# Feed-forward: 42 gate and up tile pairs by a seven-product scheme, two of four weight sums by adding DMAs

## The chip, the cores and the metric

The kernel runs on one core of a Trainium2 chip. The metric is the device time of one execution in microseconds. TensorE does the matmuls, ScalarE (ACT) and VectorE (DVE) the elementwise work from SBUF and PSUM, GpSimd (POOL) elementwise work from SBUF, and SyncE (SP) issues nearly all DMAs.

## What is computed

A network on 512 tokens of width 1024, three layers in a row (a gated delta rule layer, a latent attention layer, and a second block with retention and windowed attention). Each ends in a feed-forward part with 2816 hidden columns, and the change lies in these three parts alone:

```python
def swiglu(h, w_gate, w_up, w_down):
    return (jax.nn.silu(h @ w_gate) * (h @ w_up)) @ w_down
# layers 0 and 1
h = rmsnorm(x, norm_ffn_g[layer]) * (1.0 + scale_f) + shift_f
x = x + gate_f * swiglu(h, ffn_w_gate[layer], ffn_w_up[layer], ffn_w_down[layer])
# second block (layer 2 here)
h2 = rms_norm(x, ln2_g[l])
x = x + (jax.nn.silu(h2 @ w_ffn_gate[l]) * (h2 @ w_ffn_up[l])) @ w_ffn_down[l]
```

All is float32. The kernel gets its accuracy from products of split numbers: every operand is a high half (`whi`, `hhi`) and the rest (`wlo`, `hlo`), and `mm3` (L140) makes one product of three matmuls: high by high, high by low, low by high.

## The kernel before

Activations stand transposed: eight tiles `h[k]` of 128 features by 512 tokens, each as a high and a low tile. A weight panel of 1024 by 128 columns is loaded by one DMA that SP issues (`panel`, L563) into a raw buffer `wraw` (pool `wr`, 2 buffers, L344), then split in two halves of 512: ScalarE casts to `whi` (L560), VectorE subtracts to `wlo` (L561). `whi` and `wlo` have four buffers each (pool `wp`).

`ffn` (L1170) makes a list of tiles. For each of the 22 hidden tiles c there is one of gate and one of up, each 8 k-tiles by 3 matmuls of 512 columns into one PSUM bank. `gate_done` (L1177) applies silu on ScalarE; in layer 2, where the norm is applied late (`before.late`), VectorE first scales by the norm's row and GpSimd scales again after silu (L1181 to L1183). `up_done` (L1188) multiplies on VectorE (L1191) and splits the product into `ah` and `al`. Hidden tiles come in three groups of 8, 7 and 7 (FGROUPS). After each of the first two groups stand eight tiles of the down projection over that group, added to the residual `xT` on VectorE (L637, L639). The third group's down projection is `residual` (L641), whose last four tiles and the following layer's first four run in halves of 256 tokens. The first two hidden tiles of each part are made by the stage before.

`stream` (L603) runs the list: the weights of tile i+1 are asked for inside tile i. TensorE's order is the order of the program. The orders of VectorE, ScalarE, GpSimd and SP are laid out by the framework's scheduler from a plan; each engine then works through its own order and waits where its next instruction isn't ready. In the trace the weight splits run some tiles ahead, as far as the buffers reach.

In layer 0 a side job goes along: `ada` (L542) loads 56 tiles of 512 KB into two buffers `adaw` by SP (L551) and reduces each on VectorE (L554), one step every five steps of the stream (1.6 per tile). Its sums are needed by the end of layer 0's feed-forward part and later.

## Time and profile before

| | us |
|---|---|
| median of three runs (lowest, highest) | 2250.38 (2249.84, 2254.87) |
| the profiled execution, whole | 2252.93 |
| its span, first to last instruction | 2251.1 |
| TensorE busy in the span | 2164.3 |
| VectorE, ScalarE, GpSimd busy | 1281.0, 856.2, 288.9 |

The sum of a prediction is made against the profiled execution, 2252.93 us, which is 2.55 above the median. TensorE's shown durations overlap, since matmuls are pipelined: the price of one is the distance between two starts. Durations on VectorE and ScalarE overlap a little too where instructions stand back to back.

### The profile page before, as it was taken

The numbers are of one execution on the slowest core, as the hardware profiler recorded it, in microseconds if no ns is written. First come the engines' busy times: TensorE is split into PE (matmuls) and PEld (weight loads), VectorE is DVE, ScalarE is ACT, GpSimd is POOL, SyncE is SP. The second block draws the span as 40 slices with busy tenths as digits, with TensorE's granted clock in tenths as the row PEclk, the third lists the DMA queues.
The fourth block names the chain that finished last, engine by engine and source line by source line (L and its number), as shares of the span: only waits on it lengthen the run. The fifth ranks groups of instructions, "written<-read, shape, count | busy, mean of one in ns | idle before, by whom it ended". The sixth has DMA issues, their size and how long they took to land.

```text
span 2251.1 us, 30612 instructions
## 1 busy us (share of the span) xinstructions
PE 2164.3 (96%) x11532; PEld 1830.0 (81%) x11532; DVE 1281.0 (57%) x2850; ACT 856.2 (38%) x1926; POOL 288.9 (13%) x257
## 2 busy tenths in 40 slices
PE   6997989999999999999999999999999999999998
PEld 4786777888888887688888889888778889888888
DVE  7888786577653355645333337655656654434333
ACT  4663444342222244435222234333544533323223
POOL 5331000300000031012000003212111002101012
PEclk8999999899999999999999999999999999999999
DMA  7234462267763322213332333433323242332332
GB/s 278 65 105 133 129 208 87 89 205 260 244 194 97 94 62 80 66 39 106 97 101 87 106 90 92 143 97 100 93 80 103 71 129 71 115 103 89 99 98 70
DMA packets 103235, 257.56 MB, mean 114 GB/s; under 512 B 26288, under 2 KB 36016, under 8 KB 103088
## 3 DMA queue, kind: packets, MB, share of 16 engines
q1 hardware_dynamic: 100496, 252.52, 35.9%
q10 hardware_dynamic: 2592, 3.10, 0.5%
q8 instruction: 90, 1.47, 0.3%
q14 instruction: 57, 0.47, 0.1%
HBM read 240.37 MB, written 8.91 MB: 111 GB/s over the span
## 4 chain that ended last, share of the span: by engine, by line
PE 84%; DVE 8%; DMA 3%; ACT 2%; POOL 1%; issue 1%; SPq 1%; DVEq 0%; ACTq 0%; POOLq 0%
PE ps L141 20%; PE ps L143 20%; PE ps L142 20%; PE ops L141 3%; PE ops L143 3%; PE ops L142 3%; PE first L142 1%; PE first L141 1%; PE first L143 1%; DVE wlo L561 1%; DMA adaw<-in_ada_w_dram 1%; PE mo_ps L1431 1%; PE msc L1404 1%; PE so L1564 1%; PE ssc L1525 1%
## 5 line engine op out<-in xcount | busy, mean ns | idle before, releaser
L560 ACT CAST whi<-wraw 128x512 fp32r<-128x512 f32 (+3 forms) x686 | 390.2, 605 | 926.7 <-PE ps L142 421.3
L141 PE MATMUL ps<-hhi,whi 128*128 128x512 f32 x1548 | 617.0, 399 | 17.6 <-ACT graw L1008 11.4
L143 PE MATMUL ps<-hhi,wlo 128*128 128x512 f32 x1548 | 606.7, 392 | 0.2
L142 PE MATMUL ps<-hlo,whi 128*128 128x512 f32 x1548 | 605.8, 391 | 0.8 <-DVE hlo L561 0.8
L561 DVE TENSOR_TENSOR wlo<-wraw,whi 128x512 fp32r<-128x512 f32 (+3 forms) x642 | 427.3, 694 | 173.0 <-ACT whi L560 172.1
L141 PEld LDWEIGHTS ps<-hhi,whi 128*128 128x128 f32 x1548 | 292.9, 189 | 82.5 <-ACT graw L1008 11.9
L143 PEld LDWEIGHTS ps<-hhi,wlo 128*128 128x128 f32 x1548 | 292.2, 189 | 64.8 <-DVE wlo L561 3.2
L142 PEld LDWEIGHTS ps<-hlo,whi 128*128 128x128 f32 x1548 | 292.9, 189 | 59.2 <-DVE hlo L561 1.1
L223 POOL TENSOR_TENSOR acc<-acc,sq 128x512 f32<-128x512 f32 x21 | 29.8, 1426 | 909.1 <-issue 633.9
L1191 DVE TENSOR_TENSOR far<-ps,fsg 128x512 f32<-128x512 f32 x60 | 41.5, 691 | 173.9 <-PE ps L143 172.7
L141 PE MATMUL ps<-ah,whi 128*128 128x512 f32 x360 | 140.0, 389 | 0.0
L142 PE MATMUL ps<-al,whi 128*128 128x512 f32 x360 | 140.0, 389 | 0.0
L143 PE MATMUL ps<-ah,wlo 128*128 128x512 f32 x360 | 140.0, 389 | 0.0
L554 DVE CUSTOM_DVE_ANT_0 adaw<-adaw,crow 128x1024 f32<-128x1024 f32 x80 | 97.6, 1222 | 26.1 <-DMA adaw<-in_ada_w_dram 25.9
L141 PE MATMUL first<-hhi,whi 128*128 128x256 f32 (+1 forms) x336 | 102.2, 304 | 1.3 <-ACT whi L560 1.3
L142 PE MATMUL first<-hlo,whi 128*128 128x256 f32 (+1 forms) x336 | 101.0, 301 | 1.1 <-DVE hlo L260 0.7
L143 PE MATMUL first<-hhi,wlo 128*128 128x256 f32 (+1 forms) x336 | 100.0, 298 | 1.5 <-POOL wlo L561 1.5
L141 PE MATMUL ops<-ah,whi 128*128 128x256 f32 (+1 forms) x252 | 80.4, 319 | 0.0
L142 PE MATMUL ops<-al,whi 128*128 128x256 f32 (+1 forms) x252 | 79.8, 317 | 0.0
L143 PE MATMUL ops<-ah,wlo 128*128 128x256 f32 (+1 forms) x252 | 79.8, 317 | 0.0
L141 PEld LDWEIGHTS ps<-ah,whi 128*128 128x128 f32 x360 | 67.6, 188 | 14.1
L142 PEld LDWEIGHTS ps<-al,whi 128*128 128x128 f32 x360 | 67.6, 188 | 14.0
(589 smaller groups left out, 3623.6 us busy)
## 6 DMA issues: line engine op xcount, KB each, us to landing
adaw<-in_ada_w_dram SPq DMA_DIRECT2D x96, 512.0 KB, 4.5
wraw<-in_ffn_w_gate_dram SPq DMA_DIRECT2D x44, 512.0 KB, 3.5
wraw<-in_ffn_w_up_dram SPq DMA_DIRECT2D x44, 512.0 KB, 3.5
wraw<-in_w_in_dram SPq DMA_DIRECT2D x42, 512.0 KB, 3.6
wraw<-in_gdn_w_in_dram SPq DMA_DIRECT2D x32, 512.0 KB, 3.6
wraw<-in_ffn_w_down_dram SPq DMA_DIRECT2D x32, 448.0 KB, 3.3
wraw<-in_w_ffn_gate_dram SPq DMA_DIRECT2D x22, 512.0 KB, 3.5
wraw<-in_w_ffn_up_dram SPq DMA_DIRECT2D x22, 512.0 KB, 3.5
```

The lines of the kernel that those rows point to most:

```text
L141: nc.tensor.matmul(ps, whi, hhi, start=first, stop=False)
L142: nc.tensor.matmul(ps, whi, hlo, start=False, stop=False)
L143: nc.tensor.matmul(ps, wlo, hhi, start=False, stop=last)
L223: (nc.gpsimd if half is None else nc.vector).tensor_tensor(self.acc[i][:, cols], self.acc[i][:, cols], sq, op=ALU.add)
L554: nc.vector.tensor_tensor_reduce(wt, wt, self.crow, 1.0, 0.0, ALU.mult, ALU.add, raw[:, k:k + 1])
L560: self.nc.scalar.copy(dst_hi, raw)
L561: (self.nc.gpsimd if pool else self.nc.vector).tensor_tensor(dst_lo, raw, dst_hi.bitcast(F32), op=ALU.subtract)
L1191: self.behind = nc.vector.tensor_tensor(ar, ps, sg.pop(c), op=ALU.mult).ins
L1404: nc.tensor.matmul(pss[j][:, 0:nk], qn[2 * p + j][:, qs], kn[2 * p + j][:, 0:nk], start=True, stop=False)
L1431: nc.tensor.matmul(opsum[hh][:, qs], vt, pts[j][:, CS[kj]], start=kj == 0, stop=kj == qi)
L1525: nc.tensor.matmul(sc[e][:, a:z], q[rows[e], CS[b]], c.kdup[g][rows[e], (b + 1) * P - (z - a):(b + 1) * P], start=True, stop=True)
L1564: nc.tensor.matmul(o[rows[e], CS[b]], c.vt[:, kc * P + 64 * g:kc * P + 64 * g + 64], pt[e][:, y:y + P], start=y == a, stop=y + P == z)
```

## The change

42 of the 66 gate and up pairs (12, 17 and 13 of layers 0, 1 and 2, `paired`) are no longer made as two tiles of 48 matmuls of 512 columns. They are one product of 2 x 2 blocks: the blocks are gate and up in one direction, the two halves of the 1024 features in the second, the two halves of the 512 tokens in the third. Seven products of half the features and half the tokens take the place of eight, by Winograd's form of Strassen's scheme. The sums of tokens (`token_sums`) are made once per layer, in four steps, one after each of the first separate tiles. The sums of weights (`pair_weights`) are made per pair: of the four, two by DMAs that GpSimd issues and that add what they load to `u`, two by VectorE. Then g before its sums, g after, and u after are split whole (`unit`, 1024 wide), and u's second half before its sums into buffers of its own (`ffu`, two). `two` runs the seven products and combines them from PSUM. `one` runs a tile of the old kind; side steps of `ada` are taken only in these, three per tile. The raw weight buffers become four outside the first stage, the parts for tokens and outputs get pools of their own, PSUM banks are taken from the pools of three and five apart (`self.wide = False`), and the scratch for DMA descriptors that software writes is made 2048.

```diff
@@ -341,7 +341,7 @@
     def weights(self, es, n, **k):
-        self.wr, self.wp = self.pool("wr", 2, es, **k), self.pool("wp", n, es, **k)
+        self.wr, self.wp = self.pool("wr", 2 if k else 4, es, **k), self.pool("wp", n, es, **k)
...
@@ -1167,51 +1167,198 @@
+    def pair_weights(self, w1, w2, c, pool, out):
+        nc = self.nc
+        g, u = (self.wr.tile([P, KD, P], F32, name="wraw", tag="wraw") for _ in range(2))
+        for raw, w in ((g, w1), (u, w2)):
+            nc.sync.dma_start(raw, w.tiles(0, KD, c, P)[0])
+        a, b = slice(0, KD // 2), slice(KD // 2, KD)
+        def unit(raw):
+            hl = [self.wp.tile([P, 1088], F32R, name=x, tag=x)[:, 16:1040].rearrange("p (k n) -> p k n", k=KD) for x in ("whi", "wlo")]
+            self.split(*hl, raw)
+            out.append(hl)
+        unit(g)
+        hl = [pool.tile([P, 544], F32R, name=x, tag=x)[:, 16:528].rearrange("p (k n) -> p k n", k=4) for x in ("uhi", "ulo")]
+        self.split(*hl, u[:, b])
+        out.append(hl)
+        add = lambda o, x, y: nc.vector.tensor_tensor(o, x, y, op=ALU.add)
+        for o, w in ((b, w2), (a, w1)):
+            nc.gpsimd.dma_start(u[:, o], w.tiles(0, KD // 2, c, P)[0], accum_op=ALU.add)
+        add(g[:, a], u[:, b], g[:, a])
+        add(g[:, b], g[:, a], g[:, b])
+        yield
+        unit(g)
+        yield
+        unit(u)
+        yield
+    def token_sums(self, before, pool, out):
+        nc = self.nc
+        lo, hi = HALF
+        for j in range(KD // 2):
+            x = []
+            for k in (j, j + KD // 2):
+                x.append(self.nm.tile([P, T], F32, name="sq", bufs=3))
+                if before.late:
+                    nc.scalar.activation(x[-1], self.xT[k], AF.Copy, scale=before.gain[:, k:k + 1])
+                else:
+                    nc.vector.tensor_tensor(x[-1], before.h[0][k].bitcast(F32), before.h[1][k].bitcast(F32), op=ALU.add)
+            o, e = x
+            nc.vector.tensor_tensor(o[:, lo], o[:, lo], o[:, hi], op=ALU.subtract)
+            nc.vector.tensor_tensor(o[:, hi], e[:, hi], o[:, hi], op=ALU.subtract)
+            nc.vector.scalar_tensor_tensor(e[:, hi], o[:, lo], -1.0, e[:, hi], op0=ALU.mult, op1=ALU.subtract)
+            nc.vector.scalar_tensor_tensor(e[:, lo], e[:, hi], -1.0, e[:, lo], op0=ALU.mult, op1=ALU.subtract)
+            th, tl = (pool.tile([P, 4, T // 2], F32R, name=x, tag=x) for x in ("th", "tl"))
+            for i, y in enumerate(x):
+                self.split(*(a.rearrange("p i t -> p (i t)")[:, T * i:T * (i + 1)] for a in (th, tl)), y)
+            out.append((th, tl))
+            yield
     def ffn(self, l, before, first, gate, norm, firsts, side=None):
         nc, h = self.nc, before.h
         wg, wu, wd = self.ffn_weights(l)
         with ExitStack() as es:
-            fa, fs = self.pool("ffa", 8, es), self.pool("ffs", 2, es)
-            sg, a = {}, None
+            fa, ft, fs, fu = self.pool("ffa", 8, es), self.pool("fft", 4, es), self.pool("ffs", 2, es), self.pool("ffu", 2, es)
+            sg, fo, sums = {}, {}, []
+            maker = self.token_sums(before, ft, sums)
+            def gated(x):
+                if before.late:
+                    nc.scalar.activation(x, x, AF.Silu)
+                    nc.gpsimd.tensor_tensor(x, x, before.row, op=ALU.mult)
+                else:
+                    nc.scalar.activation(x, x, AF.Silu)
+            def upper(ar, a):
+                ah, al = fa.tile([P, T], F32R, name="ah"), fa.tile([P, T], F32R, name="al")
+                self.split(ah, al, ar)
+                a[0].append(ah)
+                a[1].append(al)
             def gate_done(c):
                 def done(ps):
...
-                    sg[c] = fs.tile([P, T], F32, name="fsg")
+                    fo[c] = fs.tile([P, 2, T], F32, name="fo")
+                    sg[c] = fo[c][:, 0, :]
...
-                        nc.scalar.activation(sg[c], sg[c], AF.Silu)
-                        nc.gpsimd.tensor_tensor(sg[c], sg[c], before.row, op=ALU.mult)
+                        gated(sg[c])
...
-                    ar = fs.tile([P, T], F32, name="far")
+                    ar = fo.pop(c)[:, 1, :]
-                    ah, al = fa.tile([P, T], F32R, name="ah"), fa.tile([P, T], F32R, name="al")
...
+                    upper(ar, a)
...
-            specs = []
+            def one(w, c, x, done):
+                wt = []
+                def weights():
+                    wt.append(self.cols(w, c * P))
+                    yield
+                def run():
+                    ps, n = self.ps(), w.kn
+                    for k, _ in enumerate(self.proj(ps, wt[0], x)):
+                        if side is not None and k % 3 == 1:
+                            next(side, None)
+                        if k == n // 2 - 1:
+                            yield
+                    done(ps)
+                    if x is h:
+                        next(maker, None)
+                    yield
+                return weights, run
+            def two(c, a):
+                u = []
+                lo, hi = HALF
+                def products(ps, cols, wt, at, b):
+                    for j in range(KD // 2):
+                        mm3(nc, ps[:, cols], wt[0][:, at + j, :], wt[1][:, at + j, :], *b(j), j == 0, j == KD // 2 - 1)
+                def run():
+                    B = lambda k, cols: lambda j: [x[k + j][:, cols] for x in h]
+                    S = lambda i: lambda j: [x[:, i, :] for x in sums[j]]
+                    tt = lambda o, x, y: nc.vector.tensor_tensor(o, x, y, op=ALU.add)
+                    both = lambda x: x.rearrange("p (c t) -> p c t", c=2)
+                    twice = lambda x: x.rearrange("p (c t) -> p c t", c=1).broadcast_to([P, 2, T // 2])
+                    a_, b_ = 0, KD // 2
+                    fo = fs.tile([P, 2, T], F32, name="fo")
+                    sg, ar = fo[:, 0, :], fo[:, 1, :]
+                    p15, p26, p37, p4 = self.s("p15"), self.s("p26"), self.s("p37"), self.bank("p4")
+                    products(p15, lo, u[0], a_, B(a_, lo))
+                    products(p26, lo, u[0], b_, B(b_, lo))
+                    p1 = self.nm.tile([P, T // 2], F32, name="nt", bufs=4)
+                    nc.scalar.copy(p1, p15[:, lo])
+                    yield
+                    products(p26, hi, u[2], a_, S(3))
+                    tt(fo[:, :, lo], both(p26), twice(p1))
+                    products(p37, hi, u[3], a_, S(1))
+                    products(p37, lo, u[2], b_, B(b_, hi))
+                    yield
+                    products(p15, hi, u[3], b_, S(0))
+                    x = self.nm.tile([P, T // 2], F32, name="nt", bufs=4)
+                    tt(x, p15[:, hi], ar[:, lo])
+                    tt(fo[:, :, hi], both(p37), twice(x))
+                    tt(ar[:, lo], p37[:, hi], ar[:, lo])
+                    if before.late:
+                        nc.vector.tensor_tensor(sg, sg, before.row, op=ALU.mult)
+                    gated(sg)
+                    products(p4, lo, u[1], 0, S(2))
+                    tt(ar[:, lo], p4[:, lo], ar[:, lo])
+                    self.behind = nc.vector.scalar_tensor_tensor(ar, ar, -1.0, sg, op0=ALU.mult, op1=ALU.mult).ins
+                    upper(ar, a)
+                    yield
+                return lambda: self.pair_weights(wg, wu, c * P, fu, u), run
+            todo, paired = [], self.paired(l)
             for g, (lo, hi) in enumerate(FGROUPS):
                 a = ([], [])
                 for c in range(lo, hi):
-                    specs += [(self.w(wg, c * P), h, gate_done(c)), (self.w(wu, c * P), h, up_done(c, a))]
+                    if c < len(first) // 2:
+                        gate_done(c)(first[2 * c])
+                        up_done(c, a)(first[2 * c + 1])
+                    elif c in paired:
+                        todo.append(two(c, a))
+                    else:
+                        todo += [one(wg, c, h, gate_done(c)), one(wu, c, h, up_done(c, a))]
                 if g < len(FGROUPS) - 1:
                     for n in range(KD):
-                        specs.append((self.w(wd.rows(lo, hi), n * P), a, lambda ps, n=n: self.add_to_x(n, ps, gate)))
-            for (_, _, done), ps in zip(specs, first):
-                done(ps)
-            for n, _ in enumerate(self.stream(specs[len(first):])):
-                if side is not None and n % 5 == 0:
-                    next(side, None)
+                        todo.append(one(wd.rows(lo, hi), n, a, lambda ps, n=n: self.add_to_x(n, ps, gate)))
+            self.wide = False
+            drain(todo[0][0]())
+            for i, (_, run) in enumerate(todo):
+                more = todo[i + 1][0]() if i + 1 < len(todo) else iter(())
+                next(more, None)
+                for _ in run():
+                    next(more, None)
+                drain(more)
+            self.wide = True
             if side is not None:
                 drain(side)
                 self.rope_tables(lambda name: self.nm.tile([P, T], F32, name=name, tag="sq", bufs=3))
             norm = norm()
             return norm, self.residual(wd.rows(lo, hi), a, gate, norm, firsts)
+    def paired(self, l):
+        return {c for c in range(5, 22) if l == 1 or c % (3, 0, 5)[l] != 1}
...
@@ -1851,7 +1998,7 @@
 def kernel(**inputs):
-    nc = bacc.Bacc("TRN2", target_bir_lowering=False, num_devices=1)
+    nc = bacc.Bacc("TRN2", target_bir_lowering=False, num_devices=1, dynamic_dma_scratch_size=2048)
```

## Rows read from the trace of the kernel before

**Rows 1.** The page: busy time by engine, and the chain that ended last by engine.
```profile
PE 2164.3 (96%) x11532; PEld 1830.0 (81%) x11532; DVE 1281.0 (57%) x2850; ACT 856.2 (38%) x1926; POOL 288.9 (13%) x257
...
PE 84%; DVE 8%; DMA 3%; ACT 2%; POOL 1%; issue 1%; SPq 1%; DVEq 0%; ACTq 0%; POOLq 0%
```
**Rows 2.** Windows: stretch, its length, busy us (instructions) of each engine, clock, DMA share, GB/s.
```profile
core 0: us, PE busy (x) PEld busy (x) DVE busy (x) ACT busy (x) POOL busy (x), PEclk, DMA share, GB/s
461.00:494.00 33.00, 32.91 (x147) 26.81 (x147) 26.68 (x45) 15.85 (x28) 0.00 (x0) 1.00 0.75 249
...
461.00:761.00 300.00, 299.91 (x1325) 247.90 (x1325) 177.93 (x298) 89.48 (x163) 0.00 (x0) 1.00 0.61 197
1045.00:1344.00 299.00, 298.91 (x1318) 247.03 (x1317) 111.79 (x176) 88.12 (x161) 0.00 (x0) 1.00 0.34 101
1901.00:2200.00 299.00, 299.00 (x1318) 247.05 (x1318) 122.02 (x197) 89.52 (x161) 31.82 (x22) 1.00 0.33 101
```
**Rows 3.** Timeline, TensorE: start us, duration us. First matmuls of two tiles, 24 starts apart.
```profile
1961.10 0.39 PE L141 MATMUL ps<-hhi,whi 128*128 128x512 f32 x1
...
1966.54 0.39 PE L141 MATMUL ps<-ah,whi 128*128 128x512 f32 x1
```
**Rows 4.** Timeline, TensorE, last residual: matmuls of 256 columns, 84 starts apart.
```profile
2219.50 0.28 PE L141 MATMUL ops<-ah,whi 128*128 128x256 f32 x1
...
2229.40 0.28 PE L141 MATMUL ops<-ah,whi 128*128 128x256 f32 x1
```
**Rows 5.** Timeline, TensorE, a little later: 24 starts apart.
```profile
2237.06 0.28 PE L141 MATMUL ops<-ah,whi 128*128 128x256 f32 x1
...
2239.78 0.28 PE L141 MATMUL ops<-ah,whi 128*128 128x256 f32 x1
```
**Rows 6.** Timeline, VectorE, layer 2: start us, duration us, operations back to back.
```profile
1966.81 0.69 DVE L1191 TENSOR_TENSOR far<-ps,fsg 128x512 f32<-128x512 f32 x1 [3.62 <-PE ps L143]
1967.42 1.28 DVE L561 TENSOR_TENSOR wlo<-wraw,whi 128x512 fp32r<-128x512 f32 x2
1968.62 0.69 DVE L561 TENSOR_TENSOR al<-far,ah 128x512 fp32r<-128x512 f32 x1
```
**Rows 7.** Timeline, VectorE, layer 0: a 1024-wide operation and what follows it.
```profile
468.64 1.22 DVE L554 CUSTOM_DVE_ANT_0 adaw<-adaw,crow 128x1024 f32<-128x1024 f32 x1
...
469.79 0.69 DVE L561 TENSOR_TENSOR wlo<-wraw,whi 128x512 fp32r<-128x512 f32 x1
```
**Rows 8.** Timeline, VectorE, last residual: a 256-wide operation from PSUM and what follows.
```profile
2233.06 0.42 DVE L637 TENSOR_TENSOR xT<-ops,xT 128x256 f32<-128x256 f32 x1
2233.39 0.15 DVE L538 SCALAR_TENSOR_TENSOR rstdy<-rstdt,rstdy 128x2 f32<-128x2 f32 x1
```
**Rows 9.** Groups by line, shapes apart, VectorE: count, busy us, mean ns, idle before.
```profile
L639 DVE SCALAR_TENSOR_TENSOR xT<-ps,mod,xT 128x512 f32<-128x512 f32 x32 | 24.0, 750 | 68.4 <-PE ps L143 68.4
```
**Rows 10.** Waits of VectorE, 461 to 761 us: us in total, times, longest.
```profile
DVE adaw L554 <- DMA adaw<-in_ada_w_dram: 21.9, 29, 1.5
```
**Rows 11.** Groups by line, shapes apart, VectorE, 461 to 494 us: ada reductions.
```profile
L554 DVE CUSTOM_DVE_ANT_0 adaw<-adaw,crow 128x1024 f32<-128x1024 f32 x9 | 10.9, 1222 | 1.8 <-DMA adaw<-in_ada_w_dram 1.8
```
**Rows 12.** Waits of SP's queue, 461 to 761 us.
```profile
SPq L551 <- DVE adaraw L554: 104.6, 53, 4.7
```
**Rows 13.** Timeline, SP: start us, duration us of one DMA issue.
```profile
1984.99 0.33 SPq L571 DMA_DIRECT2D wraw<-in_w_ffn_gate_dram  x1
```
**Rows 14.** Groups by line, shapes apart, GpSimd: layer 2's scaling after silu.
```profile
L1183 POOL TENSOR_TENSOR fsg<-fsg,nrow 128x512 f32<-128x512 f32 x22 | 31.8, 1448 | 284.3 <-ACT fsg L1182 284.3
```
**Rows 15.** DMA issues: count, KB each, median us from issue to landing.
```profile
adaw<-in_ada_w_dram SPq DMA_DIRECT2D x96, 512.0 KB, 4.5
...
xT<-in_xT_dram SPq DMA_DIRECT2D x8, 256.0 KB, 2.9
...
crow<-in_c_dram SPq DMA_DIRECT2D x1, 512.0 KB, 7.4
```
**Rows 16.** Timeline, ScalarE, layer 2: casts back to back.
```profile
1966.56 1.14 ACT L560 CAST whi<-wraw 128x512 fp32r<-128x512 f32 x2 [3.77 <-issue]
1967.61 0.61 ACT L560 CAST ah<-far 128x512 fp32r<-128x512 f32 x1
```

More of the change, by code (lines that the diff above doesn't have):

```diff
@@ L1189, in done @@
                 def done(ps):
-                    ar = fs.tile([P, T], F32, name="far")
+                    ar = fo.pop(c)[:, 1, :]
                     self.behind = nc.vector.tensor_tensor(ar, ps, sg.pop(c), op=ALU.mult).ins
-                    ah, al = fa.tile([P, T], F32R, name="ah"), fa.tile([P, T], F32R, name="al")
-                    self.split(ah, al, ar)
-                    a[0].append(ah)
-                    a[1].append(al)
-                return done
-            specs = []
+                    upper(ar, a)
```

## The prediction

> **What bounds the kernel now.** I read the page first, then the windows of the three feed-forward stretches, then the TensorE timeline inside them. On the page TensorE is busy 96% of the span and carries 84% of the chain that ended last [rows 1]. A share over the whole span does not say what a change in one stage is worth, so the windows come next: in each of the three gate, up and down stretches (layer 0 from 461 to 761 us, layer 1 from 1045 to 1344, layer 2 from 1901 to 2200) TensorE is busy for all but 0.1 us of 299 to 300, at clock 1.00, which is the 2.4 GHz level [rows 2]. There, and only there, the change works, and there nothing but the number and the length of the matmuls sets the time. VectorE is the next engine: 178, 112 and 122 us busy in the same windows [rows 2].
>
> The price of a matmul is the distance between starts, not its shown duration. With 512 columns, 24 starts take 1966.54 - 1961.10 = 5.44 us, 0.2267 each [rows 3]. With 256 columns, the last part of the kernel has a stretch of 84 in a row, by chance the number that a new pair has: 2229.40 - 2219.50 = 9.90 us, 0.1179 each, a little more than half of 0.2267 [rows 4]. Another stretch of the same shape, after a short break, runs at half exactly: 2239.78 - 2237.06 = 2.72 us for 24, 0.1133 each [rows 5]. What decides between the two does not show. The slow one is what followed directly on 512-column matmuls, as in the new code, so I take it.
>
> **The change on TensorE.** A gate and up pair has 2 x 8 x 3 = 48 matmuls of 512 columns: 48 x 0.2267 = 10.88 us. The new pair has 7 products of 4 k-tiles with 3 matmuls of 256 columns each, 84: 9.90 us. Saved per pair 0.98 us, for 12 + 17 + 13 = 42 pairs 41.2 us. At the quick cadence a pair takes 9.52, and 42 x 1.36 = 57.1 us are saved. Nothing covers TensorE now, so all of it is off the path, unless something else is late. The rest of the working is about that.
>
> **The change on VectorE.** Queued back to back, a 512-column tensor operation costs 0.60 us (two from 1967.42 to 1968.62), not its 0.69 [rows 6]; a 1024-column one 1.15 [rows 7]; a 256-column one that reads PSUM 0.33 [rows 8]; a scalar_tensor_tensor of 512 lasts 0.75 against 0.69, so 0.66 [rows 6, 9]. Before, a pair has four subtractions for the low halves of weights, the product of gate and up and one subtraction for its low half: 6 x 0.60 = 3.6 us, with layer 2's row scaling 4.2. After: three 1024-wide subtractions 3.45, the one for u's second half 0.60, two additions of weights 1.20; then two 512-wide and three 256-wide combinations from PSUM 1.20 + 1.00, the final product 0.66, its low half 0.60. Together 8.7 us, in layer 2 9.3. Where an operation needs the one just before it the overlap of 0.09 is lost; some four of these give 9.1 and 9.7. The pair lasts 9.9 on TensorE. So VectorE goes from 33% to over 90% of a pair: it still hides, with 0.8 us to spare in layers 0 and 1 and 0.2 in layer 2. Over a whole stretch it is well clear, since the other tiles leave it idle: 112 + 17 x 5.5 = 206 us of 282 in layer 1. In runs of pairs a wait on VectorE can therefore show. The row nearest to such a wait is that of the ada reductions, which also stand in VectorE's order for a DMA: 21.9 us in 29 waits, 0.76 each [rows 10]. One of these per pair gives 9.9 in layer 1 and 10.5 in layer 2; runs there have at most four pairs, with separate or down tiles between them to catch up. Bounds for layer 2: 0 and 13 x 0.6 = 8 us; taken 2.
>
> **The start of layer 0.** Here VectorE is already busy 26.7 of 33 us [rows 2], with ada reductions of 1.22 us each among the rest. The new code adds there the four steps of token sums (each two 512 sums, four 256-wide operations, two subtractions: 1.2 + 1.3 + 1.2 = 3.7, in all 15 us) and the weights of the first two pairs (2 x 5.25). That is 26.7 + 15 + 10.5 = 52 us of work in 33, 19 too much. Nine ada reductions of 1.15 = 10 us [rows 11] can slide, since their sums are wanted only by the next layer, and so can the second pair's weights, 5 us; if all that slides, 4 us are left. Side steps now come three to a separate tile and none in a pair; the queue that loads weights is the one that issues the ada tiles, and it stands 104.6 us in this stretch for their buffers [rows 12], with weight loads queued behind it. The two more raw weight buffers hold against that. Bounds 0 and 19 us; taken 4.
>
> **The adding DMAs.** No row of before shows a DMA from GpSimd, nor one that adds. Issue: between the 0.33 us of an SP issue [rows 13] and the 1.45 of a GpSimd tensor operation [rows 14]; taken 1.0. Landing of 256 KB: from 2.9 us (a plain load of that size) to 7.4 (the slowest row of a load of twice that); the adding one reads both source and target, so I go by the 4.5 of a 512 KB load under traffic [rows 15]. A gain is excluded: no load is removed. They matter through one chain. u's second half may be split for pair i+1 only when pair i-1's last product has let go of its copy (two buffers). From there: VectorE's 0.33 + 0.66 for pair i-1's end and 0.69 for the subtraction, 1.7; issue 1.0; landing 4.5; two dependent additions 1.4; ScalarE's cast of 1024 columns 1.1 [rows 16]; subtraction 1.2: 10.9 us, between 8.6 and 14.3. It must be done when pair i+1 reaches its third product: one pair and 24 matmuls later, 9.9 + 2.8 = 12.7. So it hides by 1.8 us, and at the upper end misses by 1.6 in every second pair. Only a pair behind two others feels it, 11 in layer 1 and 4 in layer 2: 0 to 15 x 0.8 = 12 us; taken 1. GpSimd itself is not the limit: two issues and at most one operation of 1.45 us in 9.9.
>
> What VectorE runs in these stretches are tensor_tensor, scalar_tensor_tensor and the ada reductions [rows 6, 9, 11]. The Trainium skill's page "SBUF — State Buffer", section "SBUF: two separate sides", speaks against DMAs from GpSimd: GpSimd writes their descriptors and is locked out while VectorE runs an operation in a two-port mode; its example goes from 620 to 3100 ns. Its section "Who interferes with whom" excepts tensor_tensor, and by that the sum stays. If those operations did lock it out, 2.5 us more per landing is an estimate from that example, within the bounds already taken. By the page "DMA: Bandwidth & Descriptors", section "Anatomy of one DMA — SWDGE (gpsimd) path", 2 us plus bytes over 436 GB/s, an estimate of 2.6 us per landing, the chain hides further and the sum is the same.
>
> **The remaining edits.** ScalarE's casts, copy and silu per pair come to about 5 of 9.9 us (1.05 per 1024 columns [rows 16]): hidden; if ScalarE were late the chain above would lengthen one for one. Five sp banks against three per pair: the bank that pair i+1 takes third is free after pair i's VectorE sum behind its sixth product, four sevenths of a pair ahead, 5.6 us; a VectorE lag up to that costs nothing. The smaller scratch and the raw buffers in the other stages touch stages that don't wait for weights in these rows: 0.
>
> **Sum.** The profiled execution took 2252.9 us (span 2251.1), 2.5 above the median of 2250.4. 2252.9 - 41.2 + 4 + 2 + 1 = 2218.7, against the median **2216 us**.
>
> **The rivals.** (1) *VectorE in order, held at the additions* (slower). If the additions stand in VectorE's order ahead of the PSUM combinations, and the landing comes later than the order supposes, VectorE idles for the difference s in each pair. A pair then lasts 9.1 + s, and from s = 1.8 us on it is worse than the 10.88 of before. The whole of issue and landing would be s = 5.5, 42 x 3.7 = 156 us lost; with half of it filled by other work, s = 2.75, 42 x 1.0 = 41 lost: 2290 us. Against it: the ada waits are 0.76, not 3, so the order foresees landings well [rows 10]; for it: the kind of DMA is new. (2) *VectorE as the bound, chain at its upper end, layer 0 start unhidden*: 19 + 8 + 12 = 39 us eat the gain: 2248, no change that can be told; half of that 2229. For it: over 90% busy in runs. (3) *Quick cadence and everything hidden*: 2250.4 - 57.1 = 2193, with 5 us of stalls 2198. For it: two 256-column cadences are in the trace, and the slow one is the usual one; short stalls seem to be followed by the quick one.
>
> **How the numbers follow.** A measurement here can tell 0.3%, about 7 us, from no change. Forecast (2204 to 2231): 0.50. Rival 3: 0.12. Rival 2: 0.10 where part of the gain is left (2231 to 2243), 0.13 where none is. Rival 1: 0.15. Faster 0.72, same 0.13, slower 0.15. The range from 2196 to 2247 leaves out rival 1 and a few in a hundred below.
>
> **What would show it.** Right: 256-column starts 0.118 us apart across a pair, pairs of 9.9 us, VectorE over 85% busy in layer 1's runs of seven, TensorE without gaps. Wrong by rival 1: VectorE's additions waiting for a DMA for over 1.8 us per pair and TensorE waiting for a cast behind it. Wrong by rival 2: TensorE idle before third products, or in the first 50 us of layer 0. The forecast falls too if landings exceed 6.3 us in layer 1, or if the cadence in a pair is neither of the two.

## The result and the profile after

The changed kernel took 2283.36 us (median of 4 runs, 2279.55 to 2284.81) where the kernel before took 2250.11 beside it: a ratio of 1.0145, 95% interval [1.0131, 1.0158]. It is 33 us slower; the forecast was 2216, and the range ended at 2247. The profiled execution has a span of 2281.6 us, 30.5 more than before.

The windows of the three feed-forward stretches of the changed kernel come first (columns as in [rows 2]):

```profile
core 0: us, PE busy (x) PEld busy (x) DVE busy (x) ACT busy (x) POOL busy (x), PEclk, DMA share, GB/s
455.50:788.10 332.60, 301.78 (x1755) 268.66 (x1754) 252.19 (x411) 115.87 (x182) 21.00 (x24) 0.94 0.66 196
1071.30:1369.90 298.60, 286.19 (x1934) 262.42 (x1933) 206.72 (x309) 121.16 (x184) 29.49 (x34) 0.99 0.51 128
1926.00:2230.60 304.60, 291.54 (x1790) 260.45 (x1789) 194.54 (x288) 112.63 (x174) 54.76 (x48) 0.98 0.46 122
```

Before, each took 299.6 to 299.8 us from its first to its last tile, with TensorE never idle [rows 2]. By the forecast's 0.98 us a pair they should take 288.0, 283.0 and 286.9. Layer 0 took 332.6 (44.6 more than that), layer 1 298.6 (15.6), layer 2 304.6 (17.7), and TensorE is idle 31, 12 and 13 us in them. The rest of the kernel is 6 us shorter, nearly all of it ahead of layer 0's stretch, which starts at 455.5 us in place of 461.5. So the work on TensorE did shrink; the gain went into new waits. These are TensorE's longest waits in the three windows, in the order of the layers (total us, times, longest):

```profile
PE p L141 <- ACT whi L560: 19.0, 3, 10.5
PE p L143 <- DVE wlo L561: 6.4, 5, 1.9
PE ps L143 <- DVE wlo L561: 5.0, 3, 3.8
...
PE p L143 <- DVE wlo L561: 5.6, 8, 0.8
PE p L141 <- ACT whi L560: 5.6, 5, 1.7
...
PE p L141 <- ACT whi L560: 7.5, 3, 4.5
```

The waits of tile `p` (the pairs) are for the high and low halves of g after its sums, which the third product needs. A wait costs more than its length. In the TensorE timeline one such wait in layer 1 looks like this:

```profile
1223.35 0.39 PE L141 MATMUL p<-th,whi 128*128 128x256 f32 x1 [1.69 <-ACT whi L560]
...
1224.61 0.49 PE L143 MATMUL p<-th,wlo 128*128 128x256 f32 x1 [0.76 <-DVE wlo L561]
1224.89 0.41 PE L141 MATMUL p<-th,whi 128*128 128x256 f32 x1
1225.11 0.42 PE L142 MATMUL p<-tl,whi 128*128 128x256 f32 x1
```

And in windows of 3 us before it, behind it and later (the last three columns are the granted clock, the DMA share and GB/s):

```profile
1218.00:1221.00 3.00, 3.00 (x29) 3.00 (x28) 0.97 (x2) 0.33 (x1) 0.86 (x1) 1.00 0.91 126
1224.60:1227.60 3.00, 2.99 (x14) 3.00 (x15) 3.00 (x5) 1.90 (x4) 0.00 (x0) 0.52 0.64 188
1229.50:1232.50 3.00, 3.00 (x29) 3.00 (x28) 0.57 (x1) 0.00 (x0) 0.86 (x1) 1.00 0.55 103
```

After the two waits the granted clock is 0.52 (the 1.2 GHz level) and starts are 0.21 us apart instead of 0.11, until about 1228.2. The pair takes 14.13 us instead of 9.53: 2.9 of gaps and 1.7 of slow clock.

**Layer 1: a loop.** A run is a row of pairs with no other tile between them. The seven pairs of one run, by the starts of their first products from 1178.5 us, take 9.90, 9.53, 9.52, 11.34, 14.13, 10.77 and 12.12 us. The timelines of VectorE, ScalarE and GpSimd over one turn:

```profile
1220.72 1.42 DVE L1193 TENSOR_TENSOR wraw<-wraw 128x512 f32<-128x512 f32 x2 [1.66 <-DMA wraw<-in_ffn_w_up_dram]
...
1227.40 0.68 DVE L561 TENSOR_TENSOR ulo<-wraw,uhi 128x512 fp32r<-128x512 f32 x1
...
1233.07 1.42 DVE L1193 TENSOR_TENSOR wraw<-wraw 128x512 f32<-128x512 f32 x2 [3.00 <-DMA wraw<-in_ffn_w_up_dram]
...
1222.25 1.99 ACT L560 CAST whi<-wraw 128x1024 fp32r<-128x1024 f32 x2 [3.91 <-DVE wraw L1193]
1224.15 0.63 ACT L1240 ACTIVATE fo<-fo 128x512 f32<-128x512 f32 x1
1224.68 1.03 ACT L560 CAST whi<-wraw 128x1024 fp32r<-128x1024 f32 x1
1225.62 0.61 ACT L560 CAST uhi<-wraw 128x512 fp32r<-128x512 f32 x1
...
1228.44 0.86 POOL L1195 DMA_DIRECT2D wraw<-in_ffn_w_up_dram  x1 [9.36 <-DVE ulo L561]
```

The additions (L1193) end at 1222.14. ScalarE, in its order, makes three casts and a silu and only then `uhi` of the next pair: to 1226.23, 4.1 us. VectorE's `ulo` ends at 1228.08, 1.85. GpSimd's issue ends at 1229.30, 1.2. The landing lets the next additions start at 1233.07, 3.8, and they take 1.4. From one start of the additions to the next that is 12.35 us for a pair, where TensorE needs 9.5 to 9.9; the turns before and behind it take 12.54 and 12.11. VectorE stands 1.66 and 3.00 us at the additions; in layer 1 such waits come to 22.6 us in 12.

**Layer 0: the ada tiles.** The five longest pieces of the chain of waits between 484 and 512 us:

```profile
485.68 4.06 DMA adaw<-in_ada_w_dram
489.76 1.23 DVE adaw L554
491.02 4.21 DMA adaw<-in_ada_w_dram
496.63 7.27 DMA adaw<-in_ada_w_dram
503.93 1.22 DVE adaw L554
```

SP's and VectorE's timelines beside them:

```profile
483.94 7.42 SPq L551 DMA_DIRECT2D adaw<-in_ada_w_dram  x4
491.63 0.33 SPq L1182 DMA_DIRECT2D wraw<-in_ffn_w_up_dram  x1
493.91 3.05 SPq L551 DMA_DIRECT2D adaw<-in_ada_w_dram  x2
...
492.65 1.22 DVE L554 CUSTOM_DVE_ANT_0 adaw<-adaw,crow 128x1024 f32<-128x1024 f32 x1
493.80 0.69 DVE L561 TENSOR_TENSOR ulo<-wraw,uhi 128x512 fp32r<-128x512 f32 x1
495.37 1.22 DVE L554 CUSTOM_DVE_ANT_0 adaw<-adaw,crow 128x1024 f32<-128x1024 f32 x1 [0.88 <-DMA adaw<-in_ada_w_dram]
```

Reductions stand among the splits that pairs wait for, and a pair's load among the ada loads. The first pair starts at 496.1, 8 us later than six tiles of 5.44 from 455.5 would let it. Pairs at 496, 583, 597 and 624 us take 22.5, 13.6, 16.6 and 24.0 us; from 668.7 on, when the last ada tile is being reduced, all take 9.90. So some 20 of the 44.6 us are lost up to the first pair's end and some 24 in the three later ones.

### The profile page after: what moved, and what is told of

It reads as the page before. It is cut to its first block, busy times and chain, and to the rows that moved or that the text cites. A ratio compares the mean times of both kernels' runs of the same rounds, so it can differ in the third digit from the quotient of the medians.

```text
span 2281.6 us, 34623 instructions
## 1 busy us (share of the span) xinstructions
PE 2136.6 (94%) x13044; PEld 1870.9 (82%) x13044; DVE 1543.7 (68%) x3232; ACT 948.7 (42%) x1999; POOL 369.1 (16%) x341
## 4 chain that ended last, share of the span: by engine, by line
PE 66%; DVE 16%; DMA 9%; issue 4%; ACT 3%; POOL 1%; SPq 0%; DVEq 0%; ACTq 0%; POOLq 0%
PE ps L141 12%; PE ps L143 12%; PE ps L142 12%; DMA adaw<-in_ada_w_dram 4%; DVE wlo L561 3%; PE p L143 3%; PE ops L143 3%; PE ops L142 3%; PE ops L141 3%; PE p L141 3%; PE p L142 3%; DMA wraw<-in_ffn_w_up_dram 2%; DVE adaw L554 2%; ACT whi L560 1%; PE first L142 1%
## 5 line engine op out<-in xcount | busy, mean ns | idle before, releaser
L560 ACT CAST whi<-wraw 128x512 fp32r<-128x512 f32 (+5 forms) x644 | 418.7, 687 | 671.4 <-PE ps L142 260.7
L561 DVE TENSOR_TENSOR wlo<-wraw,whi 128x512 fp32r<-128x512 f32 (+4 forms) x600 | 473.5, 812 | 86.1 <-ACT whi L560 80.3
L141 PE MATMUL ps<-hhi,whi 128*128 128x512 f32 x876 | 356.7, 407 | 16.9 <-ACT graw L1008 11.1
L143 PE MATMUL ps<-hhi,wlo 128*128 128x512 f32 x876 | 346.8, 396 | 6.8 <-DVE wlo L561 6.8
L142 PE MATMUL ps<-hlo,whi 128*128 128x512 f32 x876 | 345.2, 394 | 0.8 <-DVE hlo L561 0.8
L141 PE MATMUL p<-th,whi 128*128 128x256 f32 x504 | 147.9, 294 | 32.1 <-ACT whi L560 32.1
L143 PE MATMUL p<-th,wlo 128*128 128x256 f32 x504 | 148.9, 295 | 14.3 <-DVE wlo L561 14.2
L142 PE MATMUL p<-tl,whi 128*128 128x256 f32 x504 | 146.4, 291 | 0.0
L141 PE MATMUL p<-hhi,whi 128*128 128x256 f32 x504 | 141.9, 282 | 0.0
L142 PE MATMUL p<-hlo,whi 128*128 128x256 f32 x504 | 141.7, 281 | 0.0
```

The lines of the kernel that those rows point to most:

```text
L141: nc.tensor.matmul(ps, whi, hhi, start=first, stop=False)
L142: nc.tensor.matmul(ps, whi, hlo, start=False, stop=False)
L143: nc.tensor.matmul(ps, wlo, hhi, start=False, stop=last)
L560: self.nc.scalar.copy(dst_hi, raw)
L561: (self.nc.gpsimd if pool else self.nc.vector).tensor_tensor(dst_lo, raw, dst_hi.bitcast(F32), op=ALU.subtract)
```

## The experiments

Three causes were set against each other: A, the loop through the adding DMA; B, layer 0's ada tiles; C, VectorE simply too full. Stage lengths in us (layers 0, 1, 2) stand with each median; they run, in TensorE's timeline of the profiled execution, from the first tile of 512 columns to the first matmul of `residual`. The kernel before took 2249.3 to 2250.3 beside them.

**Without the adding DMAs.**

```diff
-        for o, w in ((b, w2), (a, w1)):
-            nc.gpsimd.dma_start(u[:, o], w.tiles(0, KD // 2, c, P)[0], accum_op=ALU.add)
```

> The changed kernel without its two adding DMAs; two of the four sums of weights are left out, all work of VectorE, ScalarE and TensorE stays. Theory A (VectorE is held in its order at the additions, which wait for the adding DMA; the loop ulo, issue, landing, additions, cast, wlo sets the pair): layer 1 falls from 298.6 to 282-288 us, layer 2 from 304.6 to 287-293, layer 0 by about 5 only; whole 2248 to 2258. Theory B (in layer 0 the ada tiles stand ahead of the pairs' weights): layer 0 stays above 320. Theory C (VectorE alone is too full, landings do not matter): every stage as it was, 2278 to 2288.

Measured 2229.11: 311.9, 279.7, 287.6. Every pair of layers 1 and 2 takes 9.5 to 9.9, and in layer 1 one wait of TensorE is left. A holds, C falls. That layer 0 gained 20.7 was expected by neither A (5) nor B (above 320 left): there the two causes overlap.

**Without ada tiles**, and **ada tiles spread.** The two edits:

```diff
-            for k in range(KD):
+            for k in range(0 if self.dry else KD):
```

```diff
-                        if side is not None and k % 3 == 1:
+                        if side is not None and k == 1:
...
+                    if side is not None:
+                        next(side, None)
```

(the last two lines at both inner yields of a pair; `dry` is true from layer 0's feed-forward part on)

> The changed kernel without the 56 ada tiles of layer 0's feed-forward part (neither loaded nor reduced; the sums are zero). Theory B: layer 0 falls from 332.6 to 290-297, layers 1 and 2 stay; whole 2241 to 2252. Theory A alone (the adding DMAs are the cause in layer 0 too): layer 0 stays above 318; whole 2270 to 2284.

> The changed kernel with all 56 ada tiles, but taken one to a separate or down tile and two to a pair (32 + 24) in place of three to each separate or down tile and none in a pair. If it is the bunching that holds layer 0: 332.6 falls to 295-306 and the whole to 2246-2258. If it is the sum of VectorE's work in layer 0 (reductions, token sums and pairs together), the reductions now stand inside the pairs, which have no room on VectorE: layer 0 stays above 320, whole 2270 to 2290. Layers 1 and 2 unchanged under both.

Measured 2248.09 (289.1, 298.7, 306.0) and 2256.55 (294.9, 298.7, 306.6). B holds for layer 0 alone, and it is a matter of where the steps stand: spread evenly, the same 56 reductions cost this stretch 6 us more than none. In the whole they cost 8.5: the stage behind layer 0's stretch takes 288.1 us there and 284.4 without ada tiles.

**All four sums on VectorE.**

```diff
-        for o, w in ((b, w2), (a, w1)):
-            nc.gpsimd.dma_start(u[:, o], w.tiles(0, KD // 2, c, P)[0], accum_op=ALU.add)
+        add(u[:, b], u[:, b], u[:, a])
+        add(u[:, a], u[:, a], g[:, a])
```

> The changed kernel with the two DMA sums made by VectorE from the raw tiles already loaded (two more 512-column additions per pair, 1.2 us, no issue by GpSimd and no landing). Theory A: the loop loses 5.2 us and gains 1.2; pairs in runs are then set by VectorE's 10.3 (10.9 in layer 2): layer 1 288-293, layer 2 296-301, whole 2260 to 2274. Theory C: 1.2 us more for every pair that stands in a run (about 30): layer 1 310-318, whole 2305 to 2325.

Measured 2249.92: 316.5, 283.8, 296.8. More work for VectorE made the kernel 33 us faster, the strongest evidence against C. Layer 1 did better than expected: of its runs of seven only the last two pairs take over 10 us.

**u split first**, and **three buffers for its split half.**

```diff
-        unit(g)
         hl = [pool.tile([P, 544], F32R, name=x, tag=x)[:, 16:528].rearrange("p (k n) -> p k n", k=4) for x in ("uhi", "ulo")]
         self.split(*hl, u[:, b])
...
             nc.gpsimd.dma_start(u[:, o], w.tiles(0, KD // 2, c, P)[0], accum_op=ALU.add)
+        unit(g)
```

```diff
-            fa, ft, fs, fu = self.pool("ffa", 8, es), self.pool("fft", 4, es), self.pool("ffs", 2, es), self.pool("ffu", 2, es)
+            fa, ft, fs, fu = self.pool("ffa", 8, es), self.pool("fft", 4, es), self.pool("ffs", 2, es), self.pool("ffu", 3, es)
```

> The changed kernel with u's second half split, and the two adding DMAs issued, ahead of the first split of g instead of behind it; nothing else. Theory A1 (the adding DMAs come late because ulo stands late in the orders of ScalarE and VectorE): they are issued 2 to 3 us earlier against the additions, waits of 1.7 to 3.0 shrink to under 1; layer 1 falls from 298.6 to 284-291, layer 2 from 304.6 to 291-298, whole 2256 to 2268. Theory A2 (the copy of u's half is free only after the last product of the pair two before, so the order doesn't matter): layer 1 stays at 296 or more, whole 2277 to 2288.

> The changed kernel with three buffers for u's split half in place of two (the padding of some weight buffers is cut to make room). Theory A2 (the buffer holds the loop): the DMAs can be issued a pair earlier, layer 1 falls to 280-288 and layer 2 to 288-296; whole 2246 to 2262. Theory A1 (the place in the order): stages stay within 3 us of the changed kernel's, whole 2277 to 2288.

Measured 2282.34 (328.4, 303.7, 301.8) and 2266.96 (334.8, 285.0, 293.6). ScalarE's timeline in layer 1, u first:

```profile
1218.64 2.94 ACT L560 CAST whi<-wraw 128x1024 fp32r<-128x1024 f32 x3 [4.18 <-DVE wraw L1192]
1221.48 0.61 ACT L560 CAST uhi<-wraw 128x512 fp32r<-128x512 f32 x1
```

and with three buffers:

```profile
1227.75 0.62 ACT L560 CAST uhi<-wraw 128x512 fp32r<-128x512 f32 x1 [2.56 <-DMA wraw<-in_ffn_w_up_dram]
1228.28 1.04 ACT L560 CAST whi<-wraw 128x1024 fp32r<-128x1024 f32 x1
```

The first edit did not move what it was to move: `uhi` still follows three casts that wait for the additions. So it says nothing on A1. With a third buffer `uhi` waits for its own load instead, no pair in layers 1 and 2 takes over 10 us, and VectorE's wait for the adding DMA in layer 1 falls from 22.6 us to this:

```profile
DVE wraw L1193 <- DMA wraw<-in_ffn_w_up_dram: 9.6, 8, 2.2
```

The second buffer is what closes the loop (A2). Why the order follows from it was not tried.

**The additions on GpSimd.**

```diff
-        add = lambda o, x, y: nc.vector.tensor_tensor(o, x, y, op=ALU.add)
+        add = lambda o, x, y: nc.gpsimd.tensor_tensor(o, x, y, op=ALU.add)
```

> The changed kernel with the adding DMAs kept, but the two additions that wait for them made by GpSimd in place of VectorE, so that no instruction of VectorE waits for an adding DMA. Loop theory (what sets a pair in a run is the circle additions, three casts, uhi, ulo, issue, landing, additions, measured at 12.35 us): the two additions take 2 x 1.5 in place of 1.42, the circle grows to 13.9; layer 1 305-316, layer 2 308-320, whole 2292 to 2315. Holding theory (what costs is only that VectorE's other work stands behind the waiting additions): VectorE is not held and has 1.4 us less to do per pair; layer 1 281-290, layer 2 288-296, whole 2248 to 2262.

Measured 2318.04: 331.1, 316.0, 321.8. GpSimd's timeline in layer 1:

```profile
1224.19 2.65 POOL L1193 TENSOR_TENSOR wraw<-wraw 128x512 f32<-128x512 f32 x2 [1.67 <-DMA wraw<-in_ffn_w_up_dram]
...
1237.48 2.63 POOL L1193 TENSOR_TENSOR wraw<-wraw 128x512 f32<-128x512 f32 x2 [1.11 <-DMA wraw<-in_ffn_w_up_dram]
...
1251.09 2.64 POOL L1193 TENSOR_TENSOR wraw<-wraw 128x512 f32<-128x512 f32 x2 [3.28 <-DMA wraw<-in_ffn_w_up_dram]
```

The turn is 13.3 and 13.6 us, near the loop theory's 13.9, and the holding theory's 281 to 290 for layer 1 fails. But VectorE was not set free. It no longer stood at an adding DMA, and stood instead one step on, at the subtraction behind ScalarE's cast of the sums (13.2 us in the changed kernel's layer 1):

```profile
DVE wlo L561 <- ACT whi L560: 74.6, 17, 6.0
```

So the run shows that a longer circle costs more; it doesn't show that VectorE's standing is free.

**What in layer 0's ada tiles costs.** Four runs, all with the sums on VectorE and the steps bunched (layer 0 316.5 without an edit, 289.5 with spread steps): loads by GpSimd; one load for all reductions; a one-column copy in place of each reduction; and the same with each copy tied to the reduction's place.

```diff
-                nc.sync.dma_start(wt, self.I["ada_w"][layer, 8 * v + k])
+                (nc.gpsimd if self.dry else nc.sync).dma_start(wt, self.I["ada_w"][layer, 8 * v + k])
```

```diff
-                wt = self.adp.tile([P, D], F32, name="adaw", bufs=2)
-                nc.sync.dma_start(wt, self.I["ada_w"][layer, 8 * v + k])
+                wt = self.once if self.once is not None else self.adp.tile([P, D], F32, name="adaw", bufs=2)
+                if self.once is None:
+                    nc.sync.dma_start(wt, self.I["ada_w"][layer, 8 * v + k])
...
```

```diff
                 with self.tc.issue_after(self.behind):
+                    if self.dry:
+                        nc.vector.tensor_copy(raw[:, k:k + 1], wt[:, 0:1])
+                        continue
```

(the first, the second and the fourth run; in the third the copy stands outside the `with`)

> The kernel with all sums of weights on VectorE and the ada tiles bunched as in the changed kernel (layer 0 took 316.5 us there, whole 2249.9), but in layer 0's feed-forward part the ada loads are issued by GpSimd, idle there, in place of SP. Theory Q (SP stands for a free ada buffer with the pairs' weight loads queued behind it): layer 0 falls to 289-298, whole 2221 to 2233. Theory V (the reductions' own work fills VectorE) and theory W (VectorE stands in its order for an ada landing, with the pairs' splits behind it): layer 0 stays at 311-320, whole 2244 to 2255.

> The same base, all 56 reductions kept in their places, but only the first ada tile is loaded and all reductions read it (55 loads left out, so the sums are not those of the reference). VectorE has the same work, and neither SP nor VectorE waits for an ada tile. Theories Q and W: layer 0 289-298, whole 2221 to 2233. Theory V: 310-318, whole 2243 to 2253.

> The same base, all 56 ada loads by SP, but each reduction is left out and a copy of one column stands in its place (so the sums are not those of the reference); it waits for the same landing and frees the buffer. Theory V: layer 0 289-297, whole 2221 to 2232. Theory W: the copy stands in VectorE's order as the reduction did and only its 1.2 us are gone, layer 0 303-316, whole 2236 to 2250. Theory Q: SP still waits for buffers, a little less, layer 0 300-314, whole 2233 to 2248.

> As the run without reductions, but each copy of one column is tied to the same place in VectorE's order as the reduction it stands for (without that tie they had moved ahead of the feed-forward part, from 344 us on, and cost some 14 us there). All 56 loads by SP, no reductions (the sums are not those of the reference). If the reductions' work and the waits for loads each cost their own half of layer 0's loss (316.5 with both, 302.4 without loads, 289.5 spread): layer 0 301-305, whole 2232 to 2240. If the loads cost only because the reductions behind them take long, so that the work is the whole cause: layer 0 289-295, whole 2220 to 2229. If waits for landings are the larger part: 306-316, whole 2238 to 2250.

Measured, whole and layer 0: 2258.41 and 325.9; 2233.07 and 302.4; 2234.72 and 289.1; 2228.99 and 297.0. Taking the ada loads off SP's queue made it worse, so the queue (theory Q) is not the main cause. It isn't cleared either: VectorE's waits for an ada landing (455 to 680 us), 8.7 us without an edit, rose to the first of these lines, about as much as the stretch lost. The second line is the tied run's:

```profile
DVE adaw L555 <- DMA adaw<-in_ada_w_dram: 18.7, 18, 3.1
```

```profile
DVE adaraw L556 <- DMA adaw<-in_ada_w_dram: 38.0, 29, 4.1
```

In the untied run the copies had moved to 344 us and later and held the stage before by 14 us, so its 289.1 proves nothing. In the tied run VectorE waits longest for landings, and yet layer 0 loses only 7.5 against the spread order. So of 27 us, 19.5 go with the reductions' work and 14.1 with the loads; the two overlap, and the work is the larger.

**Together.** Four versions with spread ada tiles: all sums on VectorE; the two DMA sums by GpSimd's tensor operations; both adding DMAs with three buffers; one adding DMA (for u's first half, which only the last split needs) with two buffers and with three. The second has this in place of the DMAs, the fourth has the first of VectorE's additions above and one DMA:

```diff
+        for o, x in ((b, u), (a, g)):
+            nc.gpsimd.tensor_tensor(u[:, o], u[:, o], x[:, a], op=ALU.add)
```

> All sums of weights on VectorE, and the ada tiles spread (one to a separate or down tile, two to a pair). If the adding DMAs and the bunched ada tiles are two causes that add up: layer 0 290-297, layer 1 284, layer 2 297; whole 2222 to 2233. If spread reductions and 10.3 us of VectorE work per pair together are too much for layer 0: it comes out above 300, whole 2236 or more.

> As the run with VectorE's sums and spread ada tiles, but the two sums that the DMAs made are tensor operations of GpSimd on the raw tiles in SBUF (512 columns, 1.45 us each by the row of before, 2.9 a pair; in layer 2 one more of 1.45). VectorE goes back to 9.1 us per pair. If VectorE's load is what is left after the DMAs are gone: layer 1 279-283, layer 2 288-293, layer 0 287-293, whole 2212 to 2224. If GpSimd's operations are slower beside a busy VectorE, or make VectorE's slower: layer 1 284 or more, layer 2 296 or more, whole 2226 or more.

> Both adding DMAs kept, three buffers for u's split half, and the ada tiles spread. If the loop through the second buffer and the bunched ada tiles are the two causes and add up: layer 0 288-296, layer 1 285, layer 2 294; whole 2217 to 2228. If the spread ada loads lengthen the landings of the adding DMAs in layer 0: layer 0 above 300, whole 2232 or more.

> One adding DMA instead of two: the sum that the additions wait for is made by VectorE (0.6 us), the other, which only the last split of u needs, stays a DMA; ada tiles spread; two buffers. Loop theory: the landing is out of the circle, VectorE has 9.7 us per pair (10.3 in layer 2); layer 0 288-294, layer 1 279-285, layer 2 290-297; whole 2212 to 2224. If any adding DMA in front of a split costs what two did: layer 1 292 or more, whole 2230 or more.

> As the run with one adding DMA and spread ada tiles, with three buffers for u's split half. If the buffer still holds anything there: 3 to 8 us below that run. If VectorE's load is what is left: within 3 us of it.

| | us | ratio to before | layers 0, 1, 2 |
|---|---|---|---|
| VectorE's sums | 2224.52 | 0.9888 [0.9873, 0.9903] | 289.5, 283.8, 297.8 |
| GpSimd's sums | 2247.52 | 0.9990 [0.9979, 1.0001] | 293.8, 293.3, 300.1 |
| two DMAs, three buffers | 2233.69 | 0.9928 [0.9914, 0.9943] | 296.9, 284.9, 293.9 |
| one DMA, two buffers | 2225.22 | 0.9891 [0.9876, 0.9906] | 290.7, 285.6, 294.6 |
| one DMA, three buffers | 2232.37 | 0.9920 [0.9904, 0.9937] | 293.1, 287.2, 291.2 |

The first and the fourth beat the kernel before by 25 us and the changed one by 58; between the two there is no difference to be told. Spreading alone saved 26.8 us, VectorE's sums alone 33.4, and both together 58.8, so in the whole the two causes nearly add up. In layer 0 by itself they don't (37.7 and 16.1 us apart, 43.1 together), so the near sum is in part chance. With GpSimd's sums the circle is back in another form: VectorE stands at the additions for GpSimd, and the last three pairs of layer 1's runs of seven take 11.0 to 11.6 us:

```profile
DVE wraw L1193 <- POOL wraw L1195: 15.6, 12, 2.6
```

Versions with three buffers fell 6 to 7 us short: the fifth is 7.2 slower than the fourth, the third 5.7 above its expected range. The padding of weight buffers that was cut for the room goes with 424.5 to 424.8 us in the stage between layers 1 and 2, in the other runs 419.9 to 422.1, and with pairs of 9.70 to 10.00 and none of 9.52. No run cut the padding alone, so that it is the cause isn't shown. Windows of layer 1's first long run, changed kernel and VectorE's sums:

```profile
1178.00:1246.00 68.00, 63.54 (x528) 62.30 (x528) 48.67 (x70) 26.45 (x37) 8.66 (x10) 0.97 0.50 116
```

```profile
1151.00:1210.00 59.00, 57.65 (x505) 57.25 (x504) 56.70 (x88) 29.05 (x46) 0.00 (x0) 1.00 0.33 102
```

VectorE is busy 72% in the changed kernel's run of pairs and 96% in the faster one.

## Why the prediction was wrong

**TensorE's saving** held: undisturbed pairs take 9.90 us, or 9.52 from the second or third pair of a run on, against 10.88; neither cadence was new [rows 4, 5].

**VectorE hidden** held: with the same work on it and no adding DMAs layer 2 took 287.6, 0.7 over the 286.9 (taken 2 of 0 to 8). Six of its pairs ran at the quick cadence, 2.2 us less together, so the waits are nearer 2.9. With 1.2 us more per pair it took 296.8, so the margin was as thin as stated.

**The adding DMAs**, taken at 1 of 0 to 12, is the first step that failed; layers 1 and 2 lost 33 us that vanish without them. Its sizes were right (issue 0.86 for 1.0, landing by the page's groups 4.1 to 4.8 for 4.5, additions 1.4, cast 1.05):

```profile
wraw<-in_ffn_w_gate_dram POOLq DMA_DIRECT2D x29, 256.0 KB, 4.7
wraw<-in_ffn_w_up_dram POOLq DMA_DIRECT2D x29, 256.0 KB, 4.5
wraw<-in_w_ffn_gate_dram POOLq DMA_DIRECT2D x13, 256.0 KB, 4.1
wraw<-in_w_ffn_up_dram POOLq DMA_DIRECT2D x13, 256.0 KB, 4.8
```

Its shape was wrong. I laid the chain from the moment the buffer comes free to the third product, 10.9 against 12.7, with nothing in front. But `uhi` stands in ScalarE's order behind the casts that wait for the previous pair's additions. So the chain's end feeds its beginning, once per pair: 12.35 must fit into 9.5 to 9.9, not 10.9 into 12.7. I had named the term ("if ScalarE were late the chain above would lengthen one for one") and not asked what ScalarE waits for. Rival 1 had the sign and, by luck, the size: 2290 with s = 2.75, where the waits in the run shown are 1.7 to 3.0. But it put the loss on all 42 pairs, and more than half of it lies in layer 0, where it is gone without the ada tiles. It saw VectorE held at the additions, and not that the circle through ScalarE's order brings the wait back in every pair. The price of a stall also lacked the clock's part, 1.7 us of 4.6 above.

**The start of layer 0**, taken at 4 of 0 to 19, is the second and larger one: 44.6 lost in the stretch. "Nine ada reductions can slide" was the step. They did not: in the stretch's first 33 us stand 17 instructions of the reductions' line, two to a reduction, so as before nine [rows 11], the ninth cut by the window's end. This is a window on that line alone (VectorE's busy time and count, the clock, the DMA share and GB/s):

```profile
455.50:488.50 33.00, 10.62 (x17) 1.00 0.68 221
```

And more stood behind them. At three steps to a tile the six tiles ahead of the first pair ask for 18 loads: 17 reductions are made by 513 us, eight of them where the first two pairs' weights are split. Spread, five stand in the first 33 us. `issue_after` (L553) keeps a reduction from moving ahead of the latest product of gate and up; why the order doesn't put it later was not tried. The 15 us of token sums were no loss by themselves: without ada tiles the whole stretch took 289.1. And I costed only the start, while side steps went on in threes to 670 us: the 24 us of the pairs from 583 on had no term in the sum. Waits of SP's queue for ada buffers, named as the danger [rows 12], are 100.5 us after, nearly the same; taking them away did not help, but VectorE then stood longer for landings, so their share stays open.

**The remaining edits**, taken at 0, gave 6 us back ahead of layer 0's stretch. Which of them did is not known.

**The signs to look for** did their work: additions waiting over 1.8 us, TensorE idle before third products and in layer 0's first 50 us all show; "VectorE over 85% busy" in layer 1's long runs does not, 72%, which says at once that it waits rather than works. Landings over 6.3 us in layer 1 don't show either (4.2 in the median, 6.1 at most): it was not the sizes that were off.

The Trainium skill's page "DMA: Bandwidth & Descriptors", section "Anatomy of one DMA — SWDGE (gpsimd) path", gave an estimate of 2.6 us for a landing; the rows above have 4.1 to 4.8, and the measurement decides.

## What to carry to other kernels

When a step waits for its own previous turn through several engines' orders, write the circle down with every instruction that stands ahead on each engine, and compare it with the time of one turn, not of two; taking 5 us of issue and transfer out of such a circle was worth more here than 1.2 us of extra work on an engine over 90% busy. Work that "can slide" slides only if the order lets it; count what is asked for ahead of the tight place, and spread side work over the tiles that have room. A wait on TensorE can cost more than its length: here 2.9 us of gaps brought 1.7 of slow clock.

## What was not expected of the hardware

A tensor operation of GpSimd slowed one of VectorE's beside it. In the version with GpSimd's sums, timelines of both engines show:

```profile
1179.73 3.00 POOL L1195 TENSOR_TENSOR wraw<-wraw 128x512 f32<-128x512 f32 x2 [8.56 <-DVE ulo L561]
...
1180.09 1.48 DVE L1330 SCALAR_TENSOR_TENSOR fo<-fo 128x512 f32<-128x512 f32 x1
```

That operation, with both inputs in SBUF, has a median of 1473 ns there and 685 with VectorE's sums, while operations that read PSUM keep their 684. This agrees with the Trainium skill's page "SBUF — State Buffer", section "Who interferes with whom": an operation of VectorE with two inputs in SBUF contends with one of GpSimd that reads SBUF.

The 256-column cadence goes from 0.1178 to 0.1133 us at the second or third pair of an undisturbed run of three or more in the kernels with the full padding; with the cut padding no pair comes to 9.52 us. What decides is open.
